# A 32-expert layer on one core: a float32 token gather, a choice by replaced logits, one more weight slot, a branch behind all loads and another order of the last products

## The chip, the core and the metric

The kernel runs on one core of a Trainium2 chip. The metric is the device time of one execution in microseconds (us). Five engines work side by side, each through its own queue of instructions: TensorE (PE, matrix products; its weight loads are listed as PEld), VectorE (DVE), ScalarE (ACT), GpSimd (POOL) and SyncE (SP), which here issues nearly all transfers from DRAM.

## The reference, cut to what matters

All tensors are float32. 256 tokens of width 1024 pass through a first layer with four branches and a feed-forward part, then through a second layer: pooling with differential attention, cross attention, and a mixture of 32 experts, four for each token, with a normalization at the end. The change lies in the mixture:

```python
def clamped_swiglu(gu):
    gate, up = gu[..., :D_EXPERT], gu[..., D_EXPERT:]
    gate = jnp.minimum(gate, SWIGLU_LIMIT)
    up = jnp.clip(up, -SWIGLU_LIMIT, SWIGLU_LIMIT)
    return (up + 1.0) * gate * jax.nn.sigmoid(SWIGLU_ALPHA * gate)
...
    logits = (xt @ w_router + b_router).astype(jnp.float32)
    top_val, top_idx = lax.top_k(logits, TOP_K)
    gates = jax.nn.softmax(top_val, axis=-1)
...
        xb = xt[tok]
        hb = clamped_swiglu(xb @ w_gu[e] + b_gu[e])
        yb = hb @ w_down[e] + b_down[e]
        return yb * g[:, None].astype(yb.dtype)
...
        x = x + moe_ffn(rms_norm(x, ffn_norm_g[l]), w_router[l], b_router[l], w_gu[l], b_gu[l],
                        w_down[l], b_down[l])
    return rms_norm(x, final_norm_g)
```

## The kernel before

The first three quarters of a millisecond are dense products, and the change leaves them alone. From about 755 us on the kernel works through the experts, one after another, each with up to `CAP` = 64 tokens.

**Weights.** Each expert needs 12 loads of 1 MiB: eight pieces of `w_gu` and four of `w_down`. They all go through SP's queue, in program order, into a ring of slots. `SLOTS` is the ring: each letter names the memory that a slot uses, `x` two slots that are filled early, `p` six of a pool of its own, and the other letters memory that earlier stages have freed. `slot_tile` hands the slots out in turn, so a load waits for the product that read its slot one round before, and everything behind it on SP's queue waits too. There are 23 slots.

**One expert.** `gu_product` (tile `gue`, L1530) multiplies the gathered tokens by `w_gu`: 32 float32 matmuls with 64 weight columns and 512 moving columns, two of them beside each other in the array. The profile counts two records for each float32 matmul. `gu_out` copies the product out. `swiglu` (two halves, `make(0)` and `make(1)`) transposes it (`gte`, L1551) and runs a chain of DVE and ACT operations. `dn_product` (tile `dne`, L1577) does 16 matmuls with `w_down`; `hilo` (L209 and L210) splits the result in two parts, `yh` and `yl`, and `scatter` (L1587) adds them into four accumulators `acc` with eight matmuls. `turn_slots` (`ste`) turns the 0/1 matrix that says which token sits in which of the 64 places. `front(e + 1)` puts the swiglu of expert e and the scatter of expert e-1 between the pieces of the next `gu_product`, so that PE has work while DVE and ACT run.

**Gather.** Tokens are gathered by matmul with the 0/1 matrix, for two experts at once (`GR` = 2): `group` makes it, and eight `chunk`s of 128 features each (tile `xgg`, L1474) take six bfloat16 matmuls apiece, since the normalized tokens are held as three bfloat16 parts `xs` (made by POOL and ACT, L1348 to L1352). Each chunk shares one PSUM buffer, `tr`, with the others, so it waits until DVE or ACT has copied the chunk before out (L1478, L1480). The chunks of experts 0 and 1 stand between the pieces of expert 0's `gue`; all others stand between the matmuls of `dne` of every second expert.

**Head.** Router logits: `lps` (L1303), a copy by ACT, `lp` (L1309) which adds four parts and turns them, `lg`. Then the choice on DVE: the eight largest, their indices, a 0/1 tensor `oh` of 32x4 per token (L1371), its sum `selb` (L1374), on PE the places `pos_ps` (L1378 to L1380), and from them the gather's matrix `Sg` (L1449). `seed` (L1339) puts the residual into `acc` with eight records.

**Branch.** An expert with more than 64 tokens is run again for the rest by `overflow`, a piece of code behind a branch on the counts, on all engines. With this data no expert needs it. It stands behind expert 25 (`EOVER`), and before it SP waits until its transfers have landed (L1621).

**Tail.** Experts 30 and 31 stand behind the loop, then `finish` normalizes and writes. The order of instructions on an engine follows the written order, except that a scheduler moves some of them past one another.

Of the kernel before, what the change touches and what calls it, by code (L numbers as in the profile page):

```python
# [31 lines left out]
SLOTS = "xxolkmnpppgfhppdeijpcba"  # L32
# [11 lines left out]
def kernel(ctx: ExitStack, tc: tile.TileContext, A, out, probe=None, stop=None):  # L44
# [1299 lines left out]
    for h in range(2):  # L1344
# [39 lines left out]
    def gates():  # L1384
        V.reciprocal(st_[:, :, 6:7], st_[:, :, 5:6])
        for b in range(2):
            V.tensor_scalar(st_[:, b, 0:TOPK], st_[:, b, 0:TOPK], st_[:, b, 6:7], None, op0=ALU.mult)
            V.tensor_tensor(oh[:, b], oh[:, b], st_[:, b, 0:TOPK].unsqueeze(1).to_broadcast([P, NE, TOPK]),
                            op=ALU.mult)
        V.tensor_reduce(out=gate, in_=oh, axis=AX.X, op=ALU.add)  # L1390
# [350 lines left out]
```

## Time and profile before

| | us |
|---|---|
| median of 3 runs | 1704.89 (1703.57 to 1705.97) |
| the profiled execution | 1706.54 |
| its span, from the first to the last instruction | 1704.9 |
| PE busy in the span | 1611.6 (95%) |
| DVE / ACT / POOL busy | 734.3 / 516.8 / 233.6 |

Times in a trace count from the start of the span; the profiled execution is 1.64 us longer than its span. Busy times say little by themselves: a PE that is busy can still be late because it started late. The mean granted TensorE clock of the execution is 0.992 of full speed.

### The profile page before, as it was taken

The numbers are of one execution on the slowest core, as the hardware profiler recorded it, in microseconds if no ns is written. First come the engines' busy times: TensorE is split into PE (matmuls) and PEld (weight loads), VectorE is DVE, ScalarE is ACT, GpSimd is POOL, SyncE is SP. The second block draws the span as 40 slices with busy tenths as digits, with TensorE's granted clock in tenths as the row PEclk, the third lists the DMA queues.
The fourth block names the chain that finished last, engine by engine and source line by source line (L and its number), as shares of the span: only waits on it lengthen the run. The fifth ranks groups of instructions, "written<-read, shape, count | busy, mean of one in ns | idle before, by whom it ended". The sixth has DMA issues, their size and how long they took to land. (4 is left out here: it accounts for less than half of the span.)

```text
span 1704.9 us, 24097 instructions
## 1 busy us (share of the span) xinstructions
PE 1611.6 (95%) x9539; PEld 987.2 (58%) x9540; DVE 734.3 (43%) x1606; ACT 516.8 (30%) x973; POOL 233.6 (14%) x332
## 2 busy tenths in 40 slices
PE   8899999999999999998999999999999999989896
PEld 8877799989999888973333333333333333323332
DVE  5967664567777766552322231222122312112122
ACT  4465554555555565541101110111011100101011
POOL 6988412201001100021000000000000000000000
PEclk9999999999999999999999999999999999999999
DMA  9842355655554535687999999999999999989996
GB/s 284 265 162 63 112 185 182 212 189 201 176 183 170 187 116 188 233 338 305 421 421 420 421 421 421 420 422 421 420 422 421 422 420 421 421 358 417 421 420 278
DMA packets 166420, 527.66 MB, mean 310 GB/s; under 512 B 13649, under 2 KB 101758, under 8 KB 117246
## 3 DMA queue, kind: packets, MB, share of 16 engines
q1 hardware_dynamic: 166302, 526.06, 79.9%
q8 instruction: 77, 1.26, 0.3%
q14 instruction: 41, 0.34, 0.1%
HBM read 524.95 MB, written 4.22 MB: 310 GB/s over the span
## 5 line engine op out<-in xcount | busy, mean ns | idle before, releaser
L1530 PE MATMUL gue<-raw,xgg 128*64 128x512 f32 x2032 | 461.3, 599 | 3.8 <-DMA raw<-in_w_gu_dram 3.8
L185 DVE TENSOR_TENSOR wl<-raw,wh 128x1024 fp32r<-128x1024 f32 (+3 forms) x218 | 273.3, 1255 | 179.2 <-ACT wh L184 178.7
L184 ACT CAST wh<-raw 128x1024 fp32r<-128x1024 f32 (+2 forms) x220 | 227.8, 1035 | 257.1 <-PE g L193 63.6
L1530 PEld LDWEIGHTS gue<-raw,xgg 128*64 128x64 f32 x2032 | 136.4, 137 | 263.2 <-issue 237.0
L1577 PE MATMUL dne<-raw,x_t 128*64 128x512 f32 x1024 | 242.3, 602 | 2.3 <-SPq L1621 1.1
L1478 DVE TENSOR_SCALAR xgg<-xgg,v_c 128x128 f32<-128x128 f32 x120 | 42.1, 351 | 302.8 <-PE gue L1530 173.1
L1538 ACT COPY x_t<-gue 128x512 f32<-128x512 f32 x62 | 36.3, 585 | 321.3 <-PE gue L1530 321.3
L1705 POOL TENSOR_TENSOR ssl<-ssl,nhalf 128x1 f32<-128x1 f32 x2 | 1.1, 562 | 927.5 <-DVE ssl L1704 927.5
L1577 PEld LDWEIGHTS dne<-raw,x_t 128*64 128x64 f32 x1024 | 65.2, 136 | 106.8 <-issue 91.5
L1557 DVE TENSOR_TENSOR x_t<-gte,bgu 128x256 f32<-128x256 f32 x62 | 26.3, 425 | 226.5 <-PE gte L1551 183.9
L1474 PEld LDWEIGHTS <-xs 128*128 128x128 bf16 x768 | 46.3, 98 | 105.1 <-issue 103.0
L1474 PE MATMUL xgg<-Sg,xs 128*128 128x128 bf16 x768 | 65.1, 221 | 30.9 <-DVE xgg L1478 25.0
L209 ACT ACTIVATE yh<-dne,gslote 128x512 fp32r<-128x512 f32 x32 | 22.0, 687 | 232.4 <-PE dne L1577 232.4
L379 POOL TENSOR_TENSOR convo<-convo,prod 128x256 f32<-128x256 f32 x90 | 76.8, 854 | 7.4
L192 PE MATMUL g<-h_h,wh 128*128 128x256 f32 x256 | 73.1, 286 | 0.0
L193 PE MATMUL g<-h_l,wh 128*128 128x256 f32 x256 | 73.1, 285 | 0.0
L194 PE MATMUL g<-h_h,wl 128*128 128x256 f32 x256 | 72.9, 285 | 0.0
L1563 ACT ACTIVATE x_t<-x_t 128x256 f32<-128x256 f32 x62 | 25.8, 417 | 144.2 <-DVE x_t L1561 144.2
L378 POOL TENSOR_SCALAR prod<-hconv,v_c 128x256 f32<-128x256 f32 x90 | 67.8, 753 | 8.6
L1551 PEld LDWEIGHTS gte<-ident,x_t 128*128 128x128 f32 x248 | 34.4, 208 | 56.8 <-issue 44.1
L1559 DVE TENSOR_TENSOR x_t<-gte,bgu 128x256 f32<-128x256 f32 x64 | 26.8, 418 | 67.3 <-PE dne L1577 67.3
L1551 PE MATMUL gte<-ident,x_t 128*128 128x128 f32 x248 | 45.7, 307 | 9.0 <-DVE x_t L1559 9.0
(808 smaller groups left out, 3065.8 us busy)
## 6 DMA issues: line engine op xcount, KB each, us to landing
raw<-in_w_gu_dram SPq DMA_DIRECT2D x254, 1024.0 KB
raw<-in_w_down_dram SPq DMA_DIRECT2D x138, 1024.0 KB
raw<-in_w_in_dram SPq DMA_DIRECT2D x32, 1024.0 KB
raw<-in_w_up_dram SPq DMA_DIRECT2D x22, 1024.0 KB
raw<-in_w_out_dram SPq DMA_DIRECT2D x8, 1024.0 KB
raw<-in_w_ckv_dram SPq DMA_DIRECT2D x8, 1024.0 KB
raw<-in_w_in_dram SPq DMA_DIRECT2D x13, 512.0 KB
raw<-in_w_br_dram SPq DMA_DIRECT2D x12, 512.0 KB
```

The lines of the kernel that those rows point to most:

```text
L184: S.copy(hi, src)
L185: last["lo"] = (eng or V).tensor_sub(lo, src, hi.bitcast(F32))
L192: PE.matmul(o, wh[:, k, :], ah[:, k, :], start=first and k == 0, stop=False)
L193: PE.matmul(o, wh[:, k, :], al[:, k, :], start=False, stop=False)
L194: PE.matmul(o, wl[:, k, :], ah[:, k, :], start=False, stop=last and k == nk - 1)
L378: G.tensor_scalar(prod[0][:, :T], hconv[:, c, k:k + T], w, 0.0, op0=ALU.mult, op1=ALU.add)
L379: G.tensor_add(convo[:, c, :], convo[:, c, :], prod[0][:, :T])
L1474: PE.matmul(po[:, :n * CAP], part[:, b, c * P:(c + 1) * P], s_[:, b, :, 0, :], start=i == 0, stop=i == 5)
L1478: V.tensor_scalar(xg[:, c, :], po[:, :n * CAP], vec["ffn"][:, c:c + 1], None, op0=ALU.mult)
L1530: PE.matmul(pgu[n][cg * CAP:(cg + 1) * CAP, :], xg[:, k, col:col + CAP], w[:, cg * D + n * 512:cg * D + (n + 1) * 512], start=k == 0, stop ...
L1551: PE.transpose(pt[:, c * P:(c + 1) * P], gs[:, every_other(4 * h + c)], ident)
L1577: PE.matmul(po[cg * CAP:(cg + 1) * CAP, :], u_[:, k // 4, k % 4, :], w[:, k % 2, cg * 512:(cg + 1) * 512], start=k == 0, stop=k == 7)
```

## The change

1. Gather: `chunk` takes two float32 matmuls (`x_t` by a 0/1 matrix that already holds 1/rms, `norm_hot`, four DVE operations for a pair of experts) in place of six of bfloat16. The three parts `xs` are gone. The 0/1 matrix for `turn_slots` is made for each expert by itself.
2. Logits: 16 small matmuls straight into the turned form; the copy, the second product and eight warming matmuls go.
3. Choice: the four largest logits are replaced by a constant (`match_replace`) and `selb` is where the result differs. Gates follow later, from exp(logit) times `selb`.
4. `seed` is split; half stands before `pos_ps`, half behind. Expert 0's chunks alternate between two PSUM buffers and between ACT and DVE.
5. A 24th slot, `A`.
6. `b_down` is loaded at expert 15, into a slot of the ring, and added at experts 15 and 16 (before: loaded at 1, added at 2 and 4).
7. The branch stands behind expert 29, with every load issued before it. The last loads come in the order `w_gu` of 31, `w_down` of 30, `w_down` of 31; before it was `w_down` of 30 first.
8. Expert 31's `gue` stands before (most of) expert 30's `dne`, whose pieces then cover expert 31's swiglu. `finish` multiplies by the gain before 1/rms is known.

```diff
-SLOTS = "xxolkmnpppgfhppdeijpcba"
+SLOTS = "xxolkmnpppgfhppdeijpcbaA"
...
-    lps = ps("lps", "y")
+    rlg = [ps(f"rlg{b}", tag) for b, tag in enumerate(("y", "sc"))]
     for k in range(8):
-        PE.matmul(lps[(k % 4) * NE:(k % 4 + 1) * NE, :T], wr[:, k, :], hT[:, k, :], start=k < 4, stop=k >= 4,
-                  tile_position=(0, (k % 4) * NE))
-    lsb = pn.tile([P, T], F32, tag="ahi", name="lsb")
-    S.copy(lsb, lps[:, :T])
-    lp2 = ps("lp2", "sc")
-    for b in range(2):
-        PE.matmul(lp2[:, b * NE:(b + 1) * NE], lsb[:, b * P:(b + 1) * P], ident4, start=True, stop=True)
+        for b in range(2):
+            PE.matmul(rlg[b][:, :NE], hT[:, k, b * P:(b + 1) * P], wr[:, k, :], start=k == 0, stop=k == 7)
     rm = rstd2(ss, 1e-5, const.tile([P, 2], F32, name="rm"))
-    warm(8, "tr")
...
-    xsp = [mp.tile([P, 2, D], BF16, name=f"xs{i}") for i in range(3)]
-    xr = small.tile([P, D], F32, tag="xg", name="xr", bufs=1)
-    for h in range(2):
-        for b in range(2):
-            hi, mid, lo = (t[:, b, half(h)] for t in xsp)
-            rest = xr[:, half(b)]
-            G.tensor_scalar(rest, x_t[:, b, half(h)], rm[:, b:b + 1], 0.0, op0=ALU.mult, op1=ALU.add)
-            S.copy(hi, rest)
-            G.tensor_tensor(rest, rest, hi, op=ALU.subtract)
-            S.copy(mid, rest)
-            G.tensor_tensor(lo, rest, mid, op=ALU.subtract)
...
-    for b in range(2):
-        V.max_index(i8[:, b, :], t8[:, b, :], lg[:, b, :])
-        S.activation(st_[:, b, 0:TOPK], t8[:, b, 0:TOPK], AF.Exp, bias=st_[:, b, 4:5],
-                     accum_out=st_[:, b, 5:6])
-    V.tensor_copy(fi, i8[:, :, 0:TOPK])
...
-        V.tensor_tensor(oh[:, b], iota_e.unsqueeze(2).to_broadcast([P, NE, TOPK]),
-                        fi[:, b, :].unsqueeze(1).to_broadcast([P, NE, TOPK]), op=ALU.is_equal)
+    V.memset(t8[:, :, TOPK:], 3.0e38)
+    for b in range(2):
+        V.match_replace(out=lx[:, b, :], in_to_replace=t8[:, b, :], in_values=lg[:, b, :], imm_value=-3.0e38)
     with nc.allow_low_precision(reason="0 or 1"):
-        V.tensor_reduce(out=selb, in_=oh, axis=AX.X, op=ALU.add)
+        V.tensor_tensor(selb, lx, lg, op=ALU.not_equal)
+    seed(0)
...
+    def norm_hot(pos_cols, n, name):
+
+        s_ = small.tile([P, 2, n, CAP], F32, tag="SX", name=f"SX{name}", bufs=1)
+        for b in range(2):
+            for o in range(n):
+                last["V"] = V.tensor_scalar(s_[:, b, o, :], iota_s, pos_cols[:, b, o:o + 1], rm[:, b:b + 1],
+                                            op0=ALU.is_equal, op1=ALU.mult)
         return s_
...
-            i = 0
-            for part in xsp:
-                for b in range(2):
-                    PE.matmul(po[:, :n * CAP], part[:, b, c * P:(c + 1) * P],
-                              s_[:, b, :, 0, :], start=i == 0, stop=i == 5)
-                    i += 1
+            for b in range(2):
+                PE.matmul(po[:, :n * CAP], x_t[:, b, c * P:(c + 1) * P], s_[:, b].rearrange("p o s -> p (o s)"),
+                          start=b == 0, stop=b == 1)
...
-    EOVER = NE - 7
+    EOVER = NE - 3
...
-        if e == 1:
-
+        if e == 15:
             load_b_down()
+        if e == EOVER:
+
+            wg1 = load_gu(w_gu[e1])
+            wd0, wd1 = load_dn(w_dn2[e0]), load_dn(w_dn2[e1], halves=True)
...
-        if e in (2, 4):
-            add_b_down(e // 2 - 1)
-        if e == EOVER:
-            scatter()
-            overflow()
-
-
-    e0, e1 = NE - 2, NE - 1
-    wd0, wg1, wd1 = load_dn(w_dn2[e0]), load_gu(w_gu[e1]), load_dn(w_dn2[e1], halves=True)
+        if e in (15, 16):
+            add_b_down(e - 15)
+
     scatter()
+    overflow()
...
-    make(1)
     slots_of(e0)
-    dn_product(wd0, st["gslot", e0], f"e{e0}")
-    pgu = gu_product(wg1, st["xg"], (e1 % GR) * CAP, f"e{e1}", {1: [scatter]})
-    gs = gu_out(pgu, f"e{e1}")
-    make = swiglu(gs, bgu[:, :, e1], f"e{e1}")
-    make(0)
-    make(1)
-    slots_of(e1)
-    dn_product(wd1, st["gslot", e1], f"e{e1}")
+    gs = gu_out(gu_product(wg1, st["xg"], (e1 % GR) * CAP, f"e{e1}", {1: [lambda: make(1)]}), f"e{e1}")
+    u1 = slot_tile()[:, :2 * 4 * CAP].rearrange("p (h c s) -> p h c s", h=2, c=4)
+    make1 = swiglu(gs, bgu[:, :, e1], f"e{e1}", u1)
+    dn_product(wd0, st["gslot", e0], f"e{e0}", between={2: [lambda: make1(0)], 4: [lambda: make1(1)]})
+    dn_product(wd1, lambda: st["gslot", e1], f"e{e1}", u_=u1, tag="mm",
+               between={2: [scatter], 4: [lambda: slots_of(e1)]})
...
             sq(ssl, junk[:, half(h)], acc[b][h], h, b)
+            V.tensor_tensor(outs[b][:, half(1 - h)], acc[b][1 - h], gb2[:, half(1 - h)], op=ALU.mult)
```

How instructions move, as the built programs list them (a row is a line of the kernel, an operation, output <- inputs, and the size; xN joins equal ones). First PE at the head, from the logits to the first chunk. Before:

```order
L117 MATMUL warm_8415<-nhalf 128x128 x3
L1309 MATMUL lp_8409<-ident_4393,lsb 128x32 x2
L117 MATMUL warm_8415<-nhalf 128x128 x3
L1339 MATMUL acc_8486<-x_t,ident 128x512
L1339 MATMUL acc_8487<-x_t,ident 128x512
L1339 MATMUL acc_8488<-x_t,ident 128x512
L1339 MATMUL acc_8489<-x_t,ident 128x512
L1378 LDWEIGHTS stri
L1378 MATMUL pos_ps<-selb,stri 128x32
L1379 LDWEIGHTS stri
L1379 MATMUL pos_ps<-selb,stri 128x32
```

and of the change (`rlg` are the logits, L1324 is `seed`, L1344 to L1346 `pos_ps`; the first chunk follows right behind):

```order
L1296 MATMUL rlg_8392<-wr,hT 128x32
L1296 MATMUL rlg_8393<-wr,hT 128x32
L1324 MATMUL acc_8478<-x_t,ident 128x512
L1324 MATMUL acc_8479<-x_t,ident 128x512
L1344 LDWEIGHTS stri
L1344 MATMUL pos_ps<-selb,stri 128x32
L1345 LDWEIGHTS stri
L1345 MATMUL pos_ps<-selb,stri 128x32
L1346 LDWEIGHTS stri
L1346 MATMUL pos_ps<-selb,stri 128x32
L1324 MATMUL acc_8480<-x_t,ident 128x512
L1324 MATMUL acc_8481<-x_t,ident 128x512
```

The two steps of logits with `warm` between are one run of small matmuls now, and half of `seed` stands behind `pos_ps`. Next SP around the branch (`COMPARE_AND_BRANCH`). Before, the last loads ahead of it are the `w_down` pieces of expert 25 and the first two `w_gu` pieces of expert 27; the other six, `w_down` from expert 26 on and all of experts 28 to 31 stand behind it:

```order
L1497 DMA raw_12652<-in_w_down_dram 128x2048
L1497 DMA raw_12654<-in_w_down_dram 128x2048
L1497 DMA raw_12656<-in_w_down_dram 128x2048
L1497 DMA raw_12658<-in_w_down_dram 128x2048
L1620 TENSOR_LOAD cnt_i
L1620 ISA x2
L1497 DMA raw_13273<-in_w_gu_dram 128x2048
L1497 DMA raw_13275<-in_w_gu_dram 128x2048
L1621 COMPARE_AND_BRANCH
L1622 COMPARE_AND_BRANCH
L1622 UNCONDITIONAL_BRANCH x2
```

and of the change, where the last rows ahead of it are the last pieces of expert 31's `w_down`, and no load follows:

```order
L1469 DMA raw_12897<-in_w_down_dram 128x2048
L1469 DMA raw_12899<-in_w_down_dram 128x2048
L1469 DMA raw_12901<-in_w_down_dram 128x2048
L1469 DMA raw_12903<-in_w_down_dram 128x2048
L1469 DMA raw_12905<-in_w_down_dram 128x2048
L1489 DMA raw_12907<-in_w_down_dram 128x1024 x2
L1597 TENSOR_LOAD cnt_i
L1598 COMPARE_AND_BRANCH
L1599 COMPARE_AND_BRANCH
L1599 UNCONDITIONAL_BRANCH x2
```

The branch has moved past all the loads that stood behind it on SP's queue. Last PE in the tail. Before, the end of expert 30's `dne`, its scatter, and the start of expert 31's `gue` (raw_13873 is its first piece):

```order
L1577 MATMUL dne_13951<-raw_13871,x_t 64x512 x4
L1587 MATMUL acc_8486<-yh,sT 128x512
L1587 MATMUL acc_8487<-yh,sT 128x512
L1587 MATMUL acc_8488<-yh,sT 128x512
L1530 MATMUL gue_0_13970<-raw_13873,xgg_13662 64x512 x2
L1530 MATMUL gue_1_13971<-raw_13873,xgg_13662 64x512 x2
L1587 MATMUL acc_8486<-yl,sT 128x512
L1587 MATMUL acc_8487<-yl,sT 128x512
L1587 MATMUL acc_8489<-yh,sT 128x512
L1587 MATMUL acc_8488<-yl,sT 128x512
L1587 MATMUL acc_8489<-yl,sT 128x512
L1530 MATMUL gue_0_13970<-raw_13875,xgg_13662 64x512 x2
```

and of the change, from expert 30's first `dne` matmul (raw_12893 to raw_12899 are its four `w_down` pieces, raw_12877 the first `w_gu` piece of expert 31):

```order
L1551 MATMUL dne_13515<-raw_12893,u__8509 64x512
L1523 MATMUL gte_1_13471<-ident,raw_12866 128x128 x4
L1551 MATMUL dne_13515<-raw_12893,u__8509 64x512 x3
L1551 MATMUL dne_13515<-raw_12895,u__8509 64x512 x4
L1551 MATMUL dne_13515<-raw_12897,u__8509 64x512
L1502 MATMUL gue_0_13465<-raw_12877,xgg_12721 64x512 x2
L1502 MATMUL gue_1_13466<-raw_12877,xgg_12721 64x512 x2
```

and, behind the other seven w_gu pieces of expert 31 (14 more rows of `gue`):

```order
L1523 MATMUL gte_0_13520<-ident,gse_13511 128x128 x4
L1551 MATMUL dne_13515<-raw_12897,u__8509 64x512 x3
L1551 MATMUL dne_13515<-raw_12899,u__8509 64x512
L1523 MATMUL gte_1_13536<-ident,gse_13511 128x128 x4
L1551 MATMUL dne_13515<-raw_12899,u__8509 64x512 x3
L1551 MATMUL dne_13558<-raw_12901,raw_13514 64x512 x4
L1561 MATMUL acc_8478<-yh,sT 128x512
L1561 MATMUL acc_8479<-yh,sT 128x512
```

Nine of the 16 `dne` rows of expert 30, on its first three `w_down` pieces, still stand ahead of expert 31's `gue` in the queue, with half of `gte`; seven stand behind it, around expert 31's `gte`.

## Rows read from the trace of the kernel before

**Rows 1.** Stretches: busy us (instructions) of PE, PEld, DVE, ACT, POOL; clock; DMA share; GB/s.
```profile
760.00:775.00 15.00, 9.03 (x45) 5.00 (x46) 12.62 (x30) 6.28 (x15) 10.83 (x10) 0.84 0.43 169
775.00:780.00 5.00, 5.00 (x28) 1.61 (x26) 0.00 (x0) 0.73 (x2) 0.00 (x0) 0.81 0.43 151
850.00:1490.00 640.00, 604.93 (x3174) 224.87 (x3175) 150.85 (x427) 68.67 (x135) 0.00 (x0) 1.00 1.01 421
1520.00:1540.00 20.00, 13.62 (x55) 4.53 (x54) 4.32 (x12) 1.10 (x2) 0.00 (x0) 0.83 0.70 276
1680.00:1690.00 10.00, 7.67 (x38) 3.07 (x40) 4.09 (x13) 2.38 (x5) 0.00 (x0) 1.00 0.80 330
```

**Rows 2.** Chain that ended last: start us, us, what.
```profile
1600.91 19.82 DMA raw<-in_w_down_dram
```

**Rows 3.** Waits of PE, 850 to 1490 us: total us, times, longest.
```profile
PE xgg L1474 <- DVE xgg L1478: 20.1, 45, 0.5
```

**Rows 4.** Timeline of PE: first chunk of experts 0, 24 and 28.
```profile
808.05 0.51 PE L1474 MATMUL xgg<-Sg,xs 128*128 128x128 bf16 x6
...
1488.82 0.49 PE L1474 MATMUL xgg<-Sg,xs 128*128 128x128 bf16 x6 [0.45 <-DVE xgg L1478]
...
1613.22 0.50 PE L1474 MATMUL xgg<-Sg,xs 128*128 128x128 bf16 x6 [0.46 <-DVE xgg L1478]
```

**Rows 5.** Timeline of PE at the head of the experts.
```profile
760.52 0.53 PE L1309 MATMUL lp<-ident,lsb 128*128 128x32 f32 x4
...
761.64 3.68 PE L1339 MATMUL acc<-x_t,ident 128*128 128x512 f32 x8
...
772.91 3.68 PE L1530 MATMUL gue<-first,xgg 128*64 128x512 f32 x8
```

**Rows 6.** Timeline of DVE, then ACT, at the head.
```profile
763.16 2.36 DVE L1371 TENSOR_TENSOR oh<-iota_e,fi 128x128 f32<-128x128 f32 x2
765.55 0.42 DVE L1374 TENSOR_REDUCE selb<-oh 128x64 bf16<-128x256 f32 x1
...
771.76 0.37 ACT L1480 ACTIVATE xgg<-xgg,v_c 128x128 f32<-128x128 f32 x1 [1.78 <-POOL xs L1352]
```

**Rows 7.** Waits of SP's queue, 740 to 800 us, then 1500 to 1545 us.
```profile
SPq L1495 <- PE gue L1530: 29.8, 10, 14.6
...
SPq L1495 <- PE lp L1309: 5.3, 1, 5.3
...
SPq L1621 <- SPq L1621: 19.4, 5, 6.7
```

**Rows 8.** Timeline of PE, one chunk and its down products (expert 18).
```profile
1319.32 0.49 PE L1474 MATMUL xgg<-Sg,xs 128*128 128x128 bf16 x6 [0.45 <-DVE xgg L1478]
1319.75 1.94 PE L1577 MATMUL dne<-raw,x_t 128*64 128x512 f32 x8
```

**Rows 9.** Timeline of PE, float32 records of 128x128: start of the program, late.
```profile
7.90 2.03 PE L295 MATMUL h_t<-h_xs,x_t 128*128 128x128 f32 x16 [1.15 <-issue]
...
1642.97 1.83 PE L1681 MATMUL gb<-ident,v_c 128*128 128x128 f32 x14
```

**Rows 10.** Timeline of PE around the branch.
```profile
1525.65 1.94 PE L1577 MATMUL dne<-raw,x_t 128*64 128x512 f32 x8 [0.44 <-SPq L1621]
...
1534.02 1.10 PE L1551 MATMUL gte<-ident,raw 128*128 128x128 f32 x4 [4.12 <-PEq L1621]
```

**Rows 11.** Timeline of PE, last two experts.
```profile
1656.52 7.09 PE L1577 MATMUL dne<-raw,x_t 128*64 128x512 f32 x32
...
1680.40 1.94 PE L1530 MATMUL gue<-raw,xgg 128*64 128x512 f32 x8 [0.55 <-DMA raw<-in_w_gu_dram]
1682.27 0.75 PE L1551 MATMUL gte<-ident,x_t 128*128 128x128 f32 x4
...
1686.91 7.08 PE L1577 MATMUL dne<-raw,x_t 128*64 128x512 f32 x30
...
1695.56 0.73 PE L1587 MATMUL acc<-yl,sT 64*128 64x512 f32 x4
```

More of the change, by code (lines that the diff above doesn't have):

```diff
@@ L1334, with seed @@
     G.tensor_copy(ident_b, ident)
-    def seed():
-        for b in range(2):
-            for h in range(2):
-                PE.matmul(acc[b][h], ident, x_t[:, b, half(h)], start=True, stop=False)
-    xsp = [mp.tile([P, 2, D], BF16, name=f"xs{i}") for i in range(3)]
-    xr = small.tile([P, D], F32, tag="xg", name="xr", bufs=1)
-    for h in range(2):
-        for b in range(2):
-            hi, mid, lo = (t[:, b, half(h)] for t in xsp)
-            rest = xr[:, half(b)]
-            G.tensor_scalar(rest, x_t[:, b, half(h)], rm[:, b:b + 1], 0.0, op0=ALU.mult, op1=ALU.add)
-            S.copy(hi, rest)
-            G.tensor_tensor(rest, rest, hi, op=ALU.subtract)
-            S.copy(mid, rest)
-            G.tensor_tensor(lo, rest, mid, op=ALU.subtract)
-    t8 = small.tile([P, 2, 8], F32, tag="t8s", name="t8s", bufs=1)
-    i8 = small.tile([P, 2, 8], U32, tag="i8s", name="i8s", bufs=1)
-    fi = small.tile([P, 2, TOPK], F32, tag="fi", name="fi", bufs=1)
-    st_ = small.tile([P, 2, 8], F32, tag="st_", name="st_", bufs=1)
-    for b in range(2):
-        V.max(out=t8[:, b, :], in_=lg[:, b, :])
-    V.tensor_scalar(st_[:, :, 4:5], t8[:, :, 0:1], -1.0, None, op0=ALU.mult)
-    for b in range(2):
-        V.max_index(i8[:, b, :], t8[:, b, :], lg[:, b, :])
-        S.activation(st_[:, b, 0:TOPK], t8[:, b, 0:TOPK], AF.Exp, bias=st_[:, b, 4:5],
-                     accum_out=st_[:, b, 5:6])
-    V.tensor_copy(fi, i8[:, :, 0:TOPK])
-    oh = small.tile([P, 2, NE, TOPK], F32, tag="SG", name="oh", bufs=1)
+    def seed(b):
+        for h in range(2):
+            PE.matmul(acc[b][h], ident, x_t[:, b, half(h)], start=True, stop=False)
+    t8 = small.tile([P, 2, 8], F32, tag="t8s", name="t8s", bufs=1)
+    lx = small.tile([P, D], F32, tag="gs", name="lx", bufs=1)[:, :2 * NE].rearrange("p (b e) -> p b e", b=2)
+    st_ = small.tile([P, 2, 4], F32, tag="st_", name="st_", bufs=1)
     selb = mp.tile([P, 2, NE], BF16, name="selb")
@@ L1384, in gates @@
     def gates():
-        V.reciprocal(st_[:, :, 6:7], st_[:, :, 5:6])
         for b in range(2):
[L1387 to L1390, printed above, removed]
+            S.activation(lx[:, b, :], lg[:, b, :], AF.Exp, bias=st_[:, b, 0:1])
+            V.scalar_tensor_tensor(gate[:, b, :], lx[:, b, :], 1.0, selb[:, b, :], op0=ALU.mult, op1=ALU.mult,
+                                   accum_out=st_[:, b, 1:2])
+        V.reciprocal(st_[:, :, 2:3], st_[:, :, 1:2])
+        for b in range(2):
+            V.tensor_scalar(gate[:, b, :], gate[:, b, :], st_[:, b, 2:3], None, op0=ALU.mult)
+        gateh = small.tile([P, 2, GR, CAP], F32, tag="SX", name="gateh", bufs=1).rearrange(
+            "p b o s -> p (b o s)")[:, :2 * NE].rearrange("p (b e) -> p b e", b=2)
         V.tensor_scalar(gateh, gate, 0.5, None, op0=ALU.mult)
-        rest = oh[:, 0].rearrange("p e k -> p (e k)")[:, :2 * NE].rearrange("p (b e) -> p b e", b=2)
+        rest = lx
         with nc.allow_low_precision(reason="three parts carry the 24 bits"):
@@ L1535, in gu_out @@
         if gs is None:
-            gs = xa[:, :D]
+            gs = small.tile([P, D], F32, tag="gs", name=f"gs{name}", bufs=1)
         for n in range(2):
@@ L1543, in every_other, with swiglu @@
         return slice(f, f + 2 * P - 1, 2)
-    def swiglu(gs, bcol, name):
+    def swiglu(gs, bcol, name, u_=u_):
         def make(h):
@@ L1566, in swiglu, with dn_product @@
         return make
-    def dn_product(wt, gslot, name, chunk=None):
-        po = ps(f"dn{name}", "y")
+    def dn_product(wt, gslot, name, chunk=None, u_=u_, tag="y", between=None):
+        po = ps(f"dn{name}", tag)
         for k in range(8):
@@ L1573, in dn_product @@
                 chunk(k, True)
+            for f in (between or {}).get(k, ()):
+                f()
             if k % 2 == 0:
@@ L1593 @@
     GR = 2
-    EOVER = NE - 7
+    EOVER = NE - 3
+    e0, e1 = NE - 2, NE - 1
     st = {}
     def group(g):
-        st["S", g] = one_hot(pos1[:, :, g * GR:(g + 1) * GR], GR, f"g{g}")
-        st["xg"], chunk = gather(st["S", g], GR, f"g{g}")
+        pos_cols = pos1[:, :, g * GR:(g + 1) * GR]
+        st["xg"], chunk = gather(norm_hot(pos_cols, GR, f"g{g}"), GR, f"g{g}")
         return chunk
@@ L1608, in slots_of @@
     def slots_of(e):
-        g, o = divmod(e, GR)
-        st["gslot", e] = turn_slots(st["S", g][:, :, o], gate3[:, :, e, :], f"e{e}")
+        st["gslot", e] = turn_slots(one_hot(pos1[:, :, e:e + 1], 1, f"e{e}")[:, :, 0], gate3[:, :, e, :], f"e{e}")
     chunk = group(0)
-    gs = front(0, {k: [lambda k=k: chunk(k + 1)] if k else [lambda: chunk(0), lambda: chunk(1)] for k in range(7)})
+    first = {k: [lambda k=k: chunk(k + 1, k % 2 == 0, ("tr", "y")[(k + 1) % 2])] for k in range(1, 7)}
+    first[0] = [lambda: chunk(0), lambda: chunk(1, True, "y")]
+    first[1].append(lambda: seed(1))
+    gs = front(0, first)
     with behind({"V": last["V"]}):
@@ L1706, in finish @@
         for h in range(2):
-            V.scalar_tensor_tensor(outs[b][:, half(h)], acc[b][h], r, gb2[:, half(h)], op0=ALU.mult, op1=ALU.mult)
-            ld(out[0, b * P:(b + 1) * P, half(h)], outs[b][:, half(h)])
+            o = outs[b][:, half(h)]
+            if b and h:
+                S.activation(o, o, AF.Copy, scale=r)
+            else:
+                V.tensor_scalar(o, o, r, None, op0=ALU.mult)
+            ld(out[0, b * P:(b + 1) * P, half(h)], o)
     scatter(True, finish)
```

49 lines of the change are left out of this document (21 added, 28 removed).

## Prediction

> **What bounds the kernel now.** I read the stretches first: what the transfers do tells where PE can be waiting for them. From 850 to 1490 us the transfers run at 421 GB/s, the highest rate that the rows show over a long stretch, and there are two holes: one from 760 to 780, and one from 1520 to 1540, where the mean is 276 [rows 1]. The first is worth (421-169)/421 x 15 + (421-151)/421 x 5 = 12.2 us of transfer, the second (421-276)/421 x 20 = 6.9 us. Together 19.1 us.
>
> Do holes in the transfers cost time? The chain that ended last is made of transfers from 1600.91 us on [rows 2], so at the end they do. In the middle PE is the later one: among its waits from 850 to 1490 there is none for a transfer, and the largest is for DVE, 20.1 us [rows 3]. This fits the paces. 1 MiB at 421 GB/s takes 2.49 us, so a pair of experts (24 loads) takes 59.8 us of transfer. PE goes from the chunks in expert 0 to those in expert 24 in 1488.82-808.05 = 680.8 us, 12 pairs at 56.7 [rows 4]. PE starts a whole ring behind, is 3 us per pair faster, and has caught up shortly after 1520. So two things end together: any time that the transfers gain comes out only as far as PE gains too, and PE has about 3 us per pair to lose.
>
> **The head.** Before, the choice is slow: `oh` takes 2.36 us from 763.16, `selb` ends at 765.97, and the first copy of a chunk waits for POOL's last `xs` until 771.76 [rows 6]; expert 0's first `gue` starts at 772.91 and takes 3.68 us for eight records [rows 5], which later take 1.94 [rows 11]. In the change `xs` is gone. The logits: the order shows 12 small matmuls, 24 records, behind the last transposes at about 757.2; at 0.53/4 us per record, as in `lp` [rows 5], they end at 760.4, about where `lp` ended; `lg` is there at 761.0. MAX8, a memset, two replacements and a comparison: no row has the replacement; its bounds are 0 and `oh`'s 1.2 each, and I take 0.3, for it passes 64 values per token where `oh` passes 256. `selb` is there at about 762.4. Half of `seed` (3.68/2 = 1.84 [rows 5]) fits in that wait on PE, the places take 0.3, a DVE step 0.3, the four operations of `norm_hot` 0.9, under which the other half of `seed` lies (to 764.8); chunk 0 takes 0.5, its copy 0.4. First `gue`: 765.9, 7.0 earlier. PE has no long rest before it, so I count its eight records at the full clock: 1.8 less. Six chunks that cost 0.08 more (below) give 0.4 back. PE is 8.2-8.4 us earlier behind expert 0; I count 8.2.
>
> Transfers: SP waited 5.3 us for `lp` with a load, and 14.6 us for the first `gue` to free slot `x` [rows 7]. Slot `A` gives one more load (2.49 us) to run under the head, and the first `gue` ends at 767.8 instead of 776.6. b, a and A last to about 768.5, and the next load needs about 1.6 us to flow after its release (before: release at 776.6, and 151 GB/s from 775 to 780 [rows 1], so the transfers ran the last 1.8 us of it): 1 us of hole stays. The stream is 11.2 us earlier.
>
> **The chunks.** Before, a chunk takes 0.43 us (start of `xgg` to start of `dne`, [rows 8]). After, it is two float32 matmuls, four records of 128 weight columns by 128 moving ones. Such records in a run: 16 in 2.03 us, 14 in 1.83 us [rows 9], 0.127 and 0.131 each, so 0.51 a chunk. The bounds: below, 0.43 as before; above, the `gte` price of 0.75 for four records with a strided input [rows 11], 0.68 from start to start. I take 0.51, since the rows of [rows 9] have the same shape and read contiguous data. 0.08 x 8 = 0.64 us a pair. `norm_hot` and the separate 0/1 matrices are DVE's, which is busy 151 of 640 us [rows 1], and lie under the matmuls. The wait for the copy of the chunk before stays.
>
> A rule of the Trainium skill speaks against this edit: TensorE: Matmul & The Clock Gate, section "Weight-path perf modes", says that the fast way to load weights is taken for types other than float32 alone; by it the four loads lie bare and a chunk is nearer the upper price. [Rows 9] speak against it: a record with its load takes 0.13 us.
>
> **The branch.** SP waited 19.4 us there for its own transfers [rows 7], which made the second hole. With every load issued ahead of it, the hole goes: 6.9 us for the stream. PE pays as before: from `dne`'s end (1525.65+1.94) to the next `gte` at 1534.02 there are 6.4 us, 4.12 of them PE's own sequencer [rows 10]; now they come behind expert 29. The mean clock there was 0.83 of full speed [rows 1]; I count nothing for that, since PE's gains there are covered below.
>
> **The end of the stream.** From 1680 the core moves 330 x 10 us = 3.3 MB [rows 1], so the last weight byte came at 1680+7.8 = 1687.8; now at 1687.8-11.2-6.9 = 1669.7.
>
> **PE up to expert 31.** Chunk 0 in expert 24: 1488.82-8.2+12 x 0.64 = 1488.3. Two more pairs at 57.4: expert 28 at 1603.0, against 1613.22 [rows 4]. To the end of expert 30's `gue` 29.8 us ([rows 4] to [rows 9]) and 0.64: 1633.4; expert 29's `dne` 7.0 (16 matmuls, 32 records [rows 11]): 1640.4; scatter and branch 6.4: 1646.8; 16 `gb` records 2.1, first `gte` 0.7, the swiglu of that half under 3.9 (before, both halves lay between 1683.0 and the long `dne` run at 1686.91 [rows 11]), I take 2.6: 1652.2. Then nine `dne` matmuls and half of `gte` stand ahead of expert 31's `gue` (4.6): 1656.8.
>
> But the ninth reads the third `w_down` piece of expert 30. Before, PE took the last `w_gu` piece of 31 at 1680.40 [rows 11] with 4 MiB still to come, that is 7.4 us before the last byte; the third `w_down` piece has 5 MiB behind it: 1669.7-7.4-2.5 = 1659.8. That, and 0.44 for its matmul, is later than 1656.8. So the stream decides, by 3.5 us: `gue` of 31 starts at 1660.3.
>
> **From there to the end.** `gue` 14.0 (64 records at 0.219, [rows 11]), `gte` 0.7, four `dne` 1.8, `gte` 0.7, three 1.3, four 1.8, eight `acc` 1.5, four 1.8, `ste` 0.3, eight 3.5, to the second half of the last scatter 1.6 (1693.99 to 1695.56 [rows 11]), then 9.34 before (to 1704.9) and 9.0 now, because the multiplication by the gain (0.7) is done early and a scaling by r takes its place. Sum 38.0: 1698.3. Expert 31's swiglu lies under expert 30's last `dne` matmuls. `b_down` at 15 costs four small loads and a slot in a stretch where the stream is ahead of PE: nothing; without that cover 2.5 us.
>
> Against the profiled execution: span 1704.9 to 1698.3, -6.6, and with 1.64 around it 1699.9. The median of the runs lies 1.65 below the profiled execution, so I forecast 1704.89-6.6 = 1698.
>
> **The rivals.**
> 1. Slower: the float32 chunk is dear. Each 0.01 us costs 120 chunks x 0.01 = 1.2 us on PE, once the 3.5 us are used up (0.54 a chunk). At 0.68: 1656.8+20.4 = 1677.2, and 38.0: 1715. Break-even with before at 0.51+10.3/120 = 0.60. For it: f32 `gte`; and a chunk here is short, with changes of weight shape at both ends. Against: [rows 9]. The rule of the Trainium skill named above would lead there.
> 2. No change: the head hole stays in part. If slot `A` or b waits for something as b and a did (5.3 us), or the first `gue` is late or runs at the low clock (3.68 [rows 5]), each microsecond moves the stream's end and the total 1:1; with 5 us 1703, which no measurement tells from before well. Removing the eight `warm` matmuls makes the low clock possible: from 760 to 775, where PE rested, the mean was 0.84, and it was 0.81 behind it [rows 1].
> 3. More: the tail order costs nothing, because the stream is faster than I make it or the scheduled order hides the wait for the third piece. Then PE's 1656.8 decides: 1694.8; with the cheaper chunk 1685 to 1690 would be the least.
> 4. Not faster in the branch: it is moved to the end where nothing runs beside it, so PE's 6.4 us and the stall of all engines are bare; with a clock of 0.83 behind it for 20 us as before [rows 1], 3.4 us on PE's 1656.8, as much as the stream's lead there; beyond that 1:1, 1699 to 1702.
>
> **How the numbers follow.** ±0.2% (3.4 us) is about what a measurement can tell from no change. My forecast with its neighbours (1695 to 1701): 0.52; rival 3 0.13; rivals 2 and 4 0.22, of which two thirds lie within 0.2%; rival 1 0.13, of which a quarter within 0.2%. Faster: 0.52+0.13+0.07 = 0.72; same 0.15+0.03 = 0.18; slower 0.10. The range: rival 1's outer part (above 1710) and rival 3's (under 1690) are left out: 1690 to 1710, and 1695 to 1701 for the likeliest alone.
>
> **What would show it.** Right: 760 to 780 at about 400 GB/s and no hole at 1520; first `gue` at 766; last weight byte at 1670; chunk to `dne` 0.51; no PE wait for a transfer before expert 30, and then one for the third `w_down` piece ahead of expert 31's `gue` at 1660. Wrong: a chunk of over 0.54, a first `gue` of 3.7 us, a wait of SP at slot `A`, or a hole elsewhere.

## The result, and the profile after

The changed kernel takes 1718.51 us (median of 4 runs, 1716.02 to 1718.69) against 1705.43 us of the kernel before beside it: a ratio of 1.0072 (95% interval 1.0059 to 1.0084). It is 13 us slower; forecast were 7 us less, with a range that ended at 1710. The profiled execution's span is 1716.9 us.

The same stretches as in [rows 1], with the first 5 us of the head by themselves ahead:

```profile
760.00:765.00 5.00, 4.65 (x17) 2.41 (x17) 1.46 (x12) 0.53 (x2) 0.00 (x0) 0.66 1.00 421
760.00:775.00 15.00, 14.64 (x64) 6.86 (x63) 4.35 (x27) 1.27 (x4) 0.00 (x0) 0.89 0.90 363
775.00:780.00 5.00, 5.00 (x26) 1.99 (x25) 0.35 (x1) 0.37 (x1) 0.00 (x0) 1.00 1.00 406
850.00:1490.00 640.00, 605.82 (x2912) 232.58 (x2908) 159.94 (x488) 67.38 (x132) 0.00 (x0) 1.00 1.01 420
1520.00:1540.00 20.00, 19.38 (x95) 6.88 (x93) 5.03 (x17) 2.38 (x5) 0.00 (x0) 1.00 1.01 421
1680.00:1690.00 10.00, 10.00 (x50) 3.24 (x48) 0.00 (x0) 0.00 (x0) 0.00 (x0) 1.00 0.00 0
```

The holes of the stream are nearly gone, as forecast. From 760 to 780 the core loses (421-363)/421 x 15 + (421-406)/421 x 5 = 2.2 us of transfer instead of 12.2, from 1520 to 1540 nothing instead of 6.9, and from 1680 on nothing is loaded any more. But the gain doesn't come out, because PE no longer waits for the stream. PE's waits from 1490 us on:

```profile
PE gb L1657 <- PEq L1598: 6.3, 1, 6.3
PE xgg L1447 <- DVE xgg L1450: 5.4, 12, 0.5
PE ste L1432 <- DVE u__8509 L1531: 1.9, 3, 0.8
PE acc L1561 <- ACT yh L209: 1.6, 2, 0.8
PE dne L1551 <- DVE u__8509 L1537: 1.3, 1, 1.3
PE gte L1523 <- DVE u__8509 L1531: 1.2, 2, 0.6
```

None of the six is for a transfer, and between 850 and 1490 us there is none either. So PE sets the end, all the way. Where it loses, in its timeline (start us, us, records; head, expert 18 as in [rows 8], expert 28 as the last row of [rows 4], tail):

```profile
761.28 3.62 PE L1324 MATMUL acc<-x_t,ident 128*128 128x512 f32 x4 [0.35 <-DVE lg__8413 L1300]
...
767.67 1.94 PE L1502 MATMUL gue<-first,xgg 128*64 128x512 f32 x8
...
1327.46 0.71 PE L1447 MATMUL xgg<-SXg,x_t 128*128 128x128 f32 x4 [0.46 <-DVE xgg L1450]
1328.11 1.94 PE L1551 MATMUL dne<-raw,u__8509 128*64 128x512 f32 x8
...
1618.30 0.71 PE L1447 MATMUL xgg<-SXg,x_t 128*128 128x128 f32 x4 [0.46 <-DVE xgg L1450]
1618.94 1.94 PE L1551 MATMUL dne<-raw,u__8509 128*64 128x512 f32 x8
...
1658.03 0.73 PE L1561 MATMUL acc<-yl,sT 64*128 64x512 f32 x4
1665.09 3.75 PE L1657 MATMUL gb<-ident,v_c 128*128 128x128 f32 x16 [6.33 <-PEq L1598]
...
1674.28 4.47 PE L1551 MATMUL dne<-raw,u__8509 128*64 128x512 f32 x16
1678.58 13.90 PE L1502 MATMUL gue<-raw,xgg 128*64 128x512 f32 x64
```

A chunk costs 1618.94-1618.30 = 0.64 us to the start of `dne`, not 0.51 (before 0.43). From expert 18 to 28, five pairs, PE takes (1618.30-1327.46)/5 = 58.2 us a pair, 1.4 to 1.7 more than before. That is still under the stream's 59.8 us a pair, but PE, which starts a whole ring behind, no longer catches up before the end. The four records of the first half of `seed` take 3.62 us, at a mean clock of 0.66 from 760 to 765. And in the tail PE stands still for 6.33 us at the branch; the 16 `gb` records behind it take 3.75 (14 took 1.83 before, [rows 9]) and 16 `dne` records 4.47, which take 3.65 later in the same trace. Behind the branch the granted clock is at the lower of its two levels, 1.2 GHz (the line has the columns of [rows 1]):

```profile
1665.00:1669.00 4.00, 3.91 (x18) 3.94 (x19) 0.26 (x2) 0.00 (x0) 0.00 (x0) 0.50 0.97 391
```

### The profile page after: what moved, and what is told of

The parts are those of the page before. It is cut to its first block, busy times and chain, and to the rows that moved or that the text cites. A ratio compares the mean times of both kernels' runs of the same rounds, so it can differ in the third digit from the quotient of the medians.

```text
span 1716.9 us, 23610 instructions
## 1 busy us (share of the span) xinstructions
PE 1635.8 (95%) x9279; PEld 1013.7 (59%) x9280; DVE 743.2 (43%) x1705; ACT 510.5 (30%) x959; POOL 220.1 (13%) x319
## 5 line engine op out<-in xcount | busy, mean ns | idle before, releaser
L1551 PE MATMUL dne<-raw,u__8509 128*64 128x512 f32 x992 | 236.3, 604 | 1.3 <-DVE u__8509 L1537 1.3
L1510 ACT COPY gse<-gue 128x512 f32<-128x512 f32 x62 | 36.3, 585 | 322.1 <-PE gue L1502 322.1
L1447 PEld LDWEIGHTS xgg<-SXg,x_t 128*128 128x128 f32 x512 | 66.7, 190 | 102.3 <-DVE xgg L1450 51.1
L1551 PEld LDWEIGHTS dne<-raw,u__8509 128*64 128x64 f32 x992 | 63.2, 136 | 101.5 <-issue 87.2
L1447 PE MATMUL xgg<-SXg,x_t 128*128 128x128 f32 x512 | 90.7, 300 | 26.1 <-DVE xgg L1450 25.0
L1529 DVE TENSOR_TENSOR gse<-gte,bgu 128x256 f32<-128x256 f32 x62 | 26.3, 424 | 199.6 <-PE gte L1523 179.6
L1535 ACT ACTIVATE gse<-gse 128x256 f32<-128x256 f32 x62 | 25.8, 416 | 148.8 <-DVE gse L1533 148.8
L1523 PEld LDWEIGHTS gte<-ident,gse 128*128 128x128 f32 x248 | 34.4, 207 | 57.7 <-issue 43.9
L1531 DVE TENSOR_TENSOR u__8509<-gte,bgu 128x256 f32<-128x256 f32 x62 | 25.9, 418 | 65.2 <-PE dne L1551 65.2
L1523 PE MATMUL gte<-ident,gse 128*128 128x128 f32 x248 | 45.9, 307 | 7.4 <-DVE u__8509 L1531 7.4
```

Source lines behind the costliest of these rows:

```text
L1447: PE.matmul(po[:, :n * CAP], x_t[:, b, c * P:(c + 1) * P], s_[:, b].rearrange("p o s -> p (o s)"), start=b == 0, stop=b == 1)
L1523: PE.transpose(pt[:, c * P:(c + 1) * P], gs[:, every_other(4 * h + c)], ident)
L1551: PE.matmul(po[cg * CAP:(cg + 1) * CAP, :], u_[:, k // 4, k % 4, :], w[:, k % 2, cg * 512:(cg + 1) * 512], start=k == 0, stop=k == 7)
```

## The experiments

Ratios are to the kernel before, beside which each ran; 1718.5 (1.0072) is the changed kernel. A difference between two experiments is one of medians, and where their ratios say otherwise, that stands beside it. The first four ask what makes PE late.

**1. Chunks two by two** (`two_buffers`). During the down products the two `mm` buffers of PSUM are free, so two chunks can follow each other without waiting for a copy:

```diff
-            if chunk:
-                chunk(k, True)
+            if chunk and k % 2 == 0:
+                chunk(k, True)
+                chunk(k + 1, True, "mm")
```

> The changed kernel, but the chunks inside the down products go two by two, back to back, on PSUM buffers of their own (tr and one of the two mm buffers, which are free there). Theory A: a float32 chunk costs PE 0.64 us from start to start instead of the 0.51 forecast (four records at 0.13 plus about 0.11 for the change from and to the 64-column matmuls), and this makes PE the later engine over all 15 pairs of experts. Then taking away the four waits of 0.45 us per pair, and some of the changes of shape, frees PE by 30 us or more, the stream of weights decides again, and the time falls to 1700 to 1706. In the trace: a pair of chunks in 1.2 us or less, and expert 31's gue waits for a transfer. Rival B: what costs is the branch in the tail and the low clock behind it; PE's pace over the pairs doesn't matter, and the time stays at 1716 to 1719.

Measured: 1705.61 us, ratio 1.0006 (0.9996 to 1.0015): 13 us back, theory A. The scheduler drew even more together: runs of three chunks and of three and a half (12 and 14 records). PE's timeline in expert 18, and at the start of expert 30's `dne`:

```profile
1301.01 1.68 PE L1447 MATMUL xgg<-SXg,x_t 128*128 128x128 f32 x12
1302.62 1.94 PE L1552 MATMUL dne<-raw,u__8509 128*64 128x512 f32 x8
1304.49 1.87 PE L1447 MATMUL xgg<-SXg,x_t 128*128 128x128 f32 x14
1306.29 1.94 PE L1552 MATMUL dne<-raw,u__8509 128*64 128x512 f32 x8
...
1658.47 1.94 PE L1552 MATMUL dne<-raw,u__8509 128*64 128x512 f32 x2 [6.32 <-DMA raw<-in_w_down_dram]
1660.35 1.12 PE L1523 MATMUL gte<-ident,raw 128*128 128x128 f32 x4
1661.40 5.09 PE L1552 MATMUL dne<-raw,u__8509 128*64 128x512 f32 x16
1666.32 13.90 PE L1502 MATMUL gue<-raw,xgg 128*64 128x512 f32 x64
```

12 records take 1302.62-1301.01 = 1.61 us, 14 take 1.80. With the 0.64 for four alone that is (1.80-0.64)/10 = 0.116 for each further record and 0.18 once per run. In a run a chunk costs 0.51 to 0.54, the forecast's price or little more; alone it costs 0.1 more. The edit also takes away the waits of 0.45 us for the copy of the chunk before, so its 13 us are not the price of the chunk alone; that price is what experiment 2 changes. The second part shows what comes next: PE, early now, stands 6.32 us for the first `w_down` piece of expert 30, while `gue` of 31, whose weights came earlier, is queued behind it.

**2. The bfloat16 chunks again** for all pairs but the first (`bf16_rest`), 23 slots, since the three parts need the room:

```diff
+            if parts:
+                for i, part in enumerate(parts):
+                    for b in range(2):
+                        PE.matmul(po[:, :n * CAP], part[:, b, c * P:(c + 1) * P], s_[:, b, :, 0, :],
+                                  start=i == b == 0, stop=i == 2 and b == 1)
+            for b in range(0 if parts else 2):
...
+    first[7] = [split]
     gs = front(0, first)
```

> The changed kernel with float32 chunks for experts 0 and 1 alone; for all other pairs the six bfloat16 matmuls of before, whose three parts POOL and ACT make under expert 0's gue, with 23 slots (the parts take the room of slot A). Theory A: chunks at 0.43 again, PE at 56.7 per pair, 25 us freed on PE; the stream decides, 1702 to 1707. Rival B: 1715 or more. Rival D, the logits, choice and seeds at the head as reason: 1715 or more.

Measured: 1707.22 us, 1.0009 (0.9999 to 1.0020). The head is the same as in the changed kernel (first `gue` at 768.01), so rival D falls as the main cause. Here too PE then waits for expert 30's `w_down`:

```profile
1662.31 1.94 PE L1558 MATMUL dne<-raw,x_t 128*64 128x512 f32 x2 [5.99 <-DMA raw<-in_w_down_dram]
```

**3. The slot of `work`** (`work_slot`). In the changed kernel `work`, into which ACT copies `gb`, gets the slot that holds expert 30's swiglu input. The copies wait for that swiglu, the two `mm` buffers stay taken, and so the scheduler put nine `dne` matmuls ahead of expert 31's `gue`. Now `u1`, needed later, gets that slot:

```diff
+    u1 = slot_tile()[:, :2 * 4 * CAP].rearrange("p (h c s) -> p h c s", h=2, c=4)
     work = slot_tile()
...
-    u1 = slot_tile()[:, :2 * 4 * CAP].rearrange("p (h c s) -> p h c s", h=2, c=4)
```

> The changed kernel, but the slot of expert 30's swiglu input goes to u1 and the next one to work, so that the copies of gb into work don't wait for that swiglu and expert 31's gue can stand ahead of expert 30's dne. Theory A: PE is the later engine, so only the idle time behind the first gte (0.85 and 1.26 us of waits for DVE) goes: 1715 to 1717. Rival C (the stream decides through the piece that dne of 30 waits for, as in the forecast): 10 us or more faster than the changed kernel, 1700 to 1708.

Measured: 1712.86 us, 1.0049 (1.0033 to 1.0065), 5.6 us less than the changed kernel (3.9 by the two ratios): more than theory A allowed, much less than rival C. Of the 6.7 us between the two profiled executions, 3.1 stand there already at expert 0's first `gue` (764.59 against 767.67), where both programs are the same: the dense stages ahead differ by that much from one execution to another. The tail gains 3.6. In it `gue` of 31 starts straight behind `gte`, so that the swiglu lies under it:

```profile
1665.72 0.72 PE L1523 MATMUL gte<-ident,raw 128*128 128x128 f32 x4
1666.36 1.93 PE L1502 MATMUL gue<-raw,xgg 128*64 128x512 f32 x6
```

**4. No branch** (`no_branch`):

```diff
     scatter()
-    overflow()
+    for _ in range(3):
+        slot_tile()
```

> The changed kernel without the branch and the code behind it (the second pass for experts with more than 64 tokens is left out; with this data it is not run). Rival B, the branch in the tail as the main reason: 13 us faster or more, 1705 or less. Theory A: PE saves the 6.3 us of its sequencer and some 2 to 3 us of low clock behind it, 1708 to 1711, still slower than before.

Measured: 1713.54 us, 1.0054 (1.0034 to 1.0073): 5 us less than the changed kernel (3.1 by the ratios, 5.0 in PE's rows from expert 28's first chunk on), less than either theory said, and rival B falls. The trace shows why it is less than the 6.3 us of PE's wait: `gue` of 31 now waits for those copies of `gb`, and takes 15.5 us instead of 13.9 behind that rest (granted clock 0.50 from 1668 to 1670):

```profile
1668.15 15.47 PE L1502 MATMUL gue<-raw,xgg 128*64 128x512 f32 x64 [2.86 <-ACT raw L1660]
```

The next four put the parts together, and test two steps that were left.

**5. Chunks two by two, and the slot** (`two_and_work`, edits 1 and 3).

> The changed kernel with both edits: chunks two by two on buffers of their own, and u1 in expert 30's slot, so that expert 31's gue stands ahead of expert 30's dne. If PE's pace over the pairs (theory A) and then the order of the tail are what is left, PE no longer stands 6.3 us waiting for the first w_down piece of expert 30, as it did with the pairs alone: expert 31's gue starts at about 1651 instead of 1666, and from there 44 us as in the run with the other slot: 1694 to 1698, faster than before by 0.4 to 0.6%. If the stream's end decides instead, 1702 to 1706 as with the pairs alone.

Measured: 1696.11 us, 0.9940 (0.9927 to 0.9953), as expected. The tail:

```profile
1645.13 3.75 PE L1659 MATMUL gb<-ident,v_c 128*128 128x128 f32 x16 [6.44 <-PEq L1599]
...
1649.67 2.52 PE L1502 MATMUL gue<-raw,xgg 128*64 128x512 f32 x6
...
1684.92 0.73 PE L1562 MATMUL acc<-yl,sT 64*128 64x512 f32 x4
```

`gue` of 31 starts at 1649.67, and from 1490 us on no single wait for a transfer is over 0.65 us. What is left is the branch: 6.44 us and, at a granted clock of 0.50 from 1645 to 1649, slow records behind it.

**6. The same with bfloat16 chunks** (`bf16_work`, edits 2 and 3).

> The six bfloat16 matmuls for all pairs but the first, 23 slots, and u1 in expert 30's slot. By the same reasoning gue of expert 31 starts at about 1655 instead of 1669: 1697 to 1701. If the stream's end decides, 1704 to 1708.

Measured: 1698.95 us, 0.9961 (0.9946 to 0.9976). That is 2.8 us more than in experiment 5, and the intervals overlap. The stream can account for it: with 23 slots it loses (421-287)/421 x 15 = 4.8 us in the head, against 2.0 in experiment 5 (experiment 5 ahead, columns of [rows 1]):

```profile
760.00:775.00 15.00, 14.97 (x61) 6.57 (x63) 3.90 (x25) 1.64 (x5) 0.00 (x0) 0.89 0.91 365
760.00:775.00 15.00, 14.99 (x63) 5.98 (x62) 4.93 (x17) 5.14 (x11) 10.19 (x10) 0.92 0.74 287
```

So no price of the gather's type shows once PE isn't late; with another number of slots and chunks that stand alone, this run doesn't compare the types by themselves.

**7. Warming matmuls back** (`warm_back`):

```diff
     rm = rstd2(ss, 1e-5, const.tile([P, 2], F32, name="rm"))
+    warm(8, "tr")
```

> The changed kernel with the eight warming matmuls of before behind the logits. Theory: the low clock at the head (four seed records 3.62 us instead of 1.84) comes from the many small matmuls and the rest ahead of them; with warming the seeds take about 1.9, expert 0's first gue is 1 to 2 us earlier, and, since PE is the later engine all the way, the time falls by as much: 1716 to 1718. Rival: the stretch is set by DVE's choice of the four largest, nothing changes: 1718 to 1719.

Measured: 1717.47 us, 1.0068 (1.0051 to 1.0084), not to be told from the changed kernel. The time is the rival's, but not for its reason, and the theory's gain doesn't come. The timeline, the granted clock from 760 to 763, then two rows of the changed kernel:

```profile
760.05 3.33 PE L117 MATMUL warm<-nhalf 128*128 128x128 f32 x14
763.17 1.98 PE L1325 MATMUL acc<-x_t,ident 128*128 128x512 f32 x4
...
767.93 1.94 PE L1503 MATMUL gue<-first,xgg 128*64 128x512 f32 x8
...
760.00:763.00 3.00, 3.00 (x16) 3.00 (x16) 1.52 (x11) 0.53 (x2) 0.00 (x0) 0.50 0.99 412
...
762.14 0.23 DVE L1340 TENSOR_TENSOR selb<-lx,lg__8413 128x64 bf16<-128x64 f32 x1
764.73 0.18 PE L1344 MATMUL pos_ps<-selb,stri 128*128 128x32 bf16 x1
```

With warming the seeds do take 1.98 us, as the theory said. But the warming itself now runs at the low clock, 3.33 us for 14 records, and the seeds wait for it, so nothing is gained. Nor does DVE's choice set the stretch: `selb` was ready early in the changed kernel, as forecast (762.37); what came late, at 764.73, were the places, behind the slow seeds.

**8. The kernel before with chunks two by two** (`before_two`, edit 1 on the kernel before).

> The kernel before, with its chunks two by two on the buffers tr and mm and nothing else changed. Theory: before, the stream of weights decides the end and PE only has to keep up, so 1.8 us less waiting per pair moves nothing: 1703 to 1706, no difference. If PE decided before: 20 us faster.

Measured: 1704.27 us, 0.9995 (0.9986 to 1.0005). Before, the stream decided, and PE's pace over the pairs had room to spare. For bfloat16 the rows give the price in a run too:

```profile
1306.58 1.46 PE L1474 MATMUL xgg<-Sg,xs 128*128 128x128 bf16 x20
1307.97 1.94 PE L1578 MATMUL dne<-raw,x_t 128*64 128x512 f32 x8
```

20 records in 1.39 us against 0.43 for six alone [rows 8]: (1.39-0.43)/14 = 0.069 each and only 0.02 once per run.

The last three price the branch. **9.** `work_nobranch`: edit 3, no branch.

> The changed kernel with u1 in expert 30's slot and without the branch and the code behind it (the second pass for experts with more than 64 tokens is left out). PE is the later engine there, so the branch costs what PE stands still (6.4 us) and the low clock behind it (gb 3.75 instead of 1.83): 8 us less than with the branch and that slot (1712.9), 1703 to 1707. If the gain is 5 us again as without the slot edit, 1707 to 1709, then the low clock costs nothing.

Measured: 1707.09 us, 1.0009 (1.0000 to 1.0018): 5.8 us less than with the branch and that slot (6.8 by the ratios), on the border of the two expectations. From expert 28's first chunk to the end of the span PE takes 1710.2-1615.25 = 94.95 us with the branch and 1706.6-1618.27 = 88.33 without (with it ahead):

```profile
1615.25 0.71 PE L1447 MATMUL xgg<-SXg,x_t 128*128 128x128 f32 x4 [0.45 <-DVE xgg L1450]
...
1618.27 0.71 PE L1447 MATMUL xgg<-SXg,x_t 128*128 128x128 f32 x4 [0.46 <-DVE xgg L1450]
```

That is 6.6 us: with PE late, the branch costs about the 6.4 us that PE stands still. What the low clock behind it costs by itself isn't shown, since PE's order in the tail differs too.

**10.** `two_work_nobranch`: edits 1 and 3, no branch.

> Chunks two by two, u1 in expert 30's slot, and no branch (the second pass is left out). With PE early the stream decides: expert 31's gue is paced by its loads to about 1657, the last w_down pieces come at about 1672: 1687 to 1691, 6 to 8 us less than with the branch (1696.1). If the branch is hidden behind waits for the stream there: 1695 to 1697.

Measured: 1689.26 us, 0.9902 (0.9882 to 0.9922), 6.9 us less than with the branch, as expected. `gue` of 31 is paced by its loads up to its last piece, taken at

```profile
1656.93 1.94 PE L1502 MATMUL gue<-raw,xgg 128*64 128x512 f32 x8 [0.55 <-DMA raw<-in_w_gu_dram]
```

**11.** `two_work_branch25`: edits 1 and 3, the branch at its old place.

```diff
-    EOVER = NE - 3
+    EOVER = NE - 7
...
+        if e == EOVER:
+            scatter()
+            overflow()
+
+    wg1 = load_gu(w_gu[e1])
+    wd0, wd1 = load_dn(w_dn2[e0]), load_dn(w_dn2[e1], halves=True)
     scatter()
-    overflow()
```

> Chunks two by two and u1 in expert 30's slot, but the branch behind expert 25 as before, with the last loads issued behind the loop in the changed order. The stream has its hole of 6.9 us again, PE has no branch at the end. If moving the branch was a gain: 1700 or more. If what the stream loses equals what PE saves at the end: 1693 to 1698, no difference from 1696.1.

Measured: 1691.20 us, 0.9918 (0.9904 to 0.9931). That is under the whole expected range, and 4.9 us under the same kernel with the branch at the end (3.8 by the ratios, whose intervals overlap a little); of the 5.1 us between the profiled executions 4.8 arise behind 1417 us. A stretch of the stream, PE behind the branch, SP's waits, and the last transfers in the chain that ended last (in one fence each):

```profile
1500.00:1520.00 20.00, 14.26 (x62) 3.82 (x58) 0.75 (x1) 1.86 (x3) 0.00 (x0) 0.99 0.80 324
1520.00:1540.00 20.00, 17.59 (x76) 6.35 (x78) 5.70 (x21) 1.20 (x3) 0.00 (x0) 0.84 0.99 407
```

```profile
1521.69 1.10 PE L1523 MATMUL gte<-ident,raw 128*128 128x128 f32 x4 [3.86 <-PEq L1599]
```

```profile
SPq L1599 <- SPq L1599: 19.4, 5, 6.8
```

```profile
1646.90 19.84 DMA raw<-in_w_down_dram
```

SP waits for its transfers as before, and the hole is (421-324)/421 x 20 + (421-407)/421 x 20 = 5.3 us. But PE stands 3.86 us instead of 6.4, and at the end, where nothing can be made up, it has no branch. The stream sets the end again, 1.9 us above the kernel without any branch (experiment 10; the intervals overlap). Of the versions that do the whole computation this is the fastest: 14 us faster than the kernel before.

## Why the prediction was wrong

- **The chunk, 0.51 us: the step that failed.** The rows that priced it [rows 9] are runs of 14 and 16 records; a chunk stands alone between 64-column matmuls, and a run of float32 records costs 0.18 us once. A bfloat16 run costs 0.02. So the edit costs 0.21 a chunk and not 0.08. It was rival 1, with a chance of 0.13 and a break-even at 0.60; 0.64 lies beyond: by that rival's own sum it alone gives 1656.8+120x0.13+38.0 = 1710.4 against 1704.9 before, and turns the gain into a loss. The price in a run was about right (0.51 to 0.54 measured). Experiments 1 and 2 bear it out from two sides: making runs (which takes away waits too), or taking bfloat16 again, gives 13 and 11 us back, and both end where PE waits for transfers.
- **What the Trainium skill said** (TensorE: Matmul & The Clock Gate, section "Weight-path perf modes": no fast weight load for float32) was weighed and set aside for [rows 9]. It pointed the right way, and the traces agree with it: the weight loads of a chunk have a mean of 190 ns in the profile of the changed kernel and 98 in that before:

```profile
L1447 PEld LDWEIGHTS xgg<-SXg,x_t 128*128 128x128 f32 x512 | 66.7, 190 | 102.3 <-DVE xgg L1450 51.1
L1474 PEld LDWEIGHTS <-xs 128*128 128x128 bf16 x768 | 46.3, 98 | 105.1 <-issue 103.0
```

  The 0.18 once per run is about one such load, as if the first load of a run lay bare. But the 0.02 of a bfloat16 run is much less than one of its loads (0.098). So what the once is made of stays open; that it is there is shown.
- **The sum by its steps.** Expert 28's chunk came at 1618.30 against 1603.0: 15.3 us late, 2.2 of it from the head (behind expert 0's `gue` PE was 6.0 us earlier than before, not 8.2). The other 13.1 arise over 14 pairs, 0.94 a pair; eight chunks at 0.13 too little make 1.04. From there to expert 31's `gue` PE took 60.3 us against 53.8: 6.5 more. From `dne`'s end to `gb`, scatter and branch took 8.6 us against 6.4 (2.2 more); `gb` and the `dne` and `gte` records ahead of `gue` ran partly at the low clock (1.5 and 2.1 more); and the stretch with expert 28's chunks took 0.7 more. The waits for the swiglu, 2.1 us, were in the sum (2.6). The stream would have held `gue` back to 3.5 us behind PE's own time in the forecast; that went unused. 15.3+6.5-3.5 = 18.3, and the remaining 38.3 us were forecast as 38.0: 1716.9 against 1698.3.
- **Right:** both holes, the choice on DVE, that before the stream decided the end (experiment 8), the tail from `gue` 31 on, and that expert 30's `w_down` holds `gue` of 31 back as soon as PE is early. In experiments 1 and 2 the wait for it stands at the first piece (6.3 and 6.0 us), not at the third as forecast; experiment 5, which has `gue` ahead of that `dne`, is rid of it.
- **The branch, 6.4 us on PE: mis-sized and misplaced.** It was taken as the same at either place, 4.12 of it PE's own sequencer. At the end this wait is 6.3 to 6.6 us in each of seven traces, at expert 25 it is 3.7 to 4.1 in three. With PE early the move itself loses 4.9 us (experiment 11; 3.8 by the ratios): the hole in the stream at expert 25 costs less than PE's stop at the end.
- **The low clock at the head** was named in rival 2 and not counted. It made the first half of `seed` 3.62 us instead of the 1.84 forecast, which is most of the head's 2.2. Warming at that place doesn't cure it (experiment 7). What brings it is open: it falls behind the 24 records of the small logit matmuls, during which PE was busy. PE's wait of 0.35 us behind them isn't the reason, for in experiment 7, without that wait, it falls too.

## What to carry to other kernels

Price an instruction by rows in the same surroundings: a price from a long run leaves out what each run costs once, and here that once (0.18 us, 120 times) was larger than the difference on which the edit was weighed. When an edit takes one bound away, ask how much the other engine has left; here PE had 3 us per pair of experts, and half of it went into the chunks. A place "behind all loads" for a stop of all engines is also the place where no later work can make it up.

## What the runs showed of the hardware

Not expected: between matmuls with 64 weight columns, a run of float32 128x128 records costs 0.18 us once and 0.116 each, a run of bfloat16 records 0.02 and 0.069. The branch, whose body isn't run, stops PE for 3.7 to 4.1 us behind expert 25 and for 6.3 to 6.6 behind expert 29; why the place matters is open. Behind it the 16 `gb` records take 3.75 us at a granted clock of 0.50. And the granted clock fell at the head (0.66 from 760 to 765) although PE was busy with small matmuls up to 0.35 us before, and in experiment 7 (0.50 from 760 to 763) without any wait.
